# A down projection's first chunk with seven block products for eight, in a hybrid decoder layer

## The chip, the cores and the metric

The kernel runs on one core of one Trainium2 chip. The metric is the device time of one execution in microseconds, the median of several runs. TensorE multiplies, VectorE, ScalarE and GpSimd compute beside it, and DMA moves data; SP's and GpSimd's queues issue the loads spoken of here.

## The reference, cut to what matters

One layer of a decoder: a mixer with state space and mLSTM heads, a cross attention over a memory, and a SwiGLU feed-forward, each between two RMS norms, for 512 prompt tokens and 8 x 8 sample tokens that share the weights. The change lies in the feed-forward:

```python
u = _rms(x) * g_pre_ffn
f = (jax.nn.silu(u @ w_gate) * (u @ w_up)) @ w_down
x = x + _rms(f) * g_post_ffn
```

`u` is 576 tokens by 1024, the hidden width is 2816 (22 tiles of 128), and the output has 1024 columns (8 tiles of 128).

## The kernel before, in words

**Numbers.** Every fp32 operand is split into a high part of reduced precision (`whi`, `hh`, `u3h`) and a low part, the rest (`wlo`, `hl`, `u3l`). A product of two operands is three matmuls of 128x128 weights: high by high, high by low, low by high. Tokens are the moving side, in two halves: 320 and 256 (HALVES), or twice 288 (EHALVES, `E`).

**Hidden tiles.** `H`, then `stores[...]`, holds hidden tiles (gate times up) as high and low parts. Tiles 0 to 3 are computed one by one inside an order written out by hand: a list of steps with positions (`at_(position, step, ...)`), sorted and issued in that order under `manual_schedule` (L2036 to L2051). `silu` (L1682), `times` (L1685) and `hidden` (L1688) are their last steps, in the scratch tile `ct`.

**Seven products for eight.** From tile 4 on, two neighbouring tiles are made together (`Pair`, L1853). The inner dimension is cut into two blocks, the two tiles are the two row blocks, the two token halves the two column blocks, and the 2x2 block product is done with seven block products instead of eight (class `Seven`, L1769, Winograd's form of Strassen's scheme). The weights need sums and differences on VectorE (`sums`, `diffs`) and their splits (`high1`, `parts2`, `parts3`, `parts4`); for two of the factors the low part is made by ScalarE (minus the raw weights) and an accumulating DMA from GpSimd's queue that adds them to the rounded ones (`low`, L1790; `place3`). Products are issued in three steps: `early`, `mid` and, behind the next pair's `early`, `late`. Between them ScalarE copies a PSUM bank (`cc`, `ct`) before a further product is accumulated into it.

**Buffers.** Raw weights have two buffers each for the first and the second tile (`raw`, `rawx`), the high and low parts three each (`whi`, `wlo`), the accumulated low parts two (`wacc`), weight sums one (`sw`). A load goes out when its buffer's last readers are done.

**Down projection, in four chunks of hidden tiles.** `Down` (L1939) does two output tiles with seven products over six hidden tiles (768 columns, blocks of three tiles), from the block sums that `Hidden.put` and `Hidden.sums` (L1924, L1928) made of the hidden tiles; `add` (L1947) adds each product to `f2`. The chunks of tiles 4 to 9 and 10 to 15 go this way. The last chunk (tiles 16 to 21) and **the first one (tiles 0 to 3)** are plain products: `down_chunk` (L1998) over eight output tiles and two token halves, weights split by `split_w` (L171; cast L179, subtraction L186), evacuated by `ev_first` (L2016, copy L2018).

**Order around the change.** By hand: tiles 0 to 3, and gate and up of tiles 4 and 5 up to `mid` of up (`pp`, positions 19 to 28.5). Then, by the order of the program and a scheduler that places instructions on each engine's queue (it may move later steps ahead on an engine): the first chunk with `late` of the pair, gate and up of tiles 6, 7 and 8, 9, gate of 10, 11, four Downs of tiles 4 to 9, up of 10, 11, and so on. Each engine works its queue in order.

Of the kernel before, what the change touches and what calls it, by code (L numbers as in the profile page):

```python
# [11 lines left out]
F32 = mybir.dt.float32  # L12
# [7 lines left out]
P = 128  # L20
# [95 lines left out]
def build(nc, tc, ctx, I, O):  # L116
# [13 lines left out]
    def SL(slot, name, dt=F32, shape=(P, KT, T)):  # L130

        return big.tile(list(shape), dt, name=name, tag="s%d" % slot, bufs=1)
# [56 lines left out]
    def split(hi, lo, src, eng=None, cast=None):  # L189
        c = (cast or A.copy)(hi, src)  # L190
        (eng or V).tensor_tensor(lo, src, hi.bitcast(F32), op=ALU.subtract)  # L191
        return c
# [843 lines left out]
    def SL0(name, dt=F32R):  # L1036
        return big0.tile([P, KT, T], dt, name=name, tag="s0", bufs=1)
# [639 lines left out]
    at_(12.9, S.dma_start, x_d, x)  # L1677


    H = []  # L1680

    def silu(j, i):  # L1682
        A.activation(ct[:, (j + i) % 2, :], B[("g", j), i], AF.Silu)

    def times(j, i):  # L1685
        V.tensor_tensor(ct[:, (j + i) % 2, :], ct[:, (j + i) % 2, :], B[("u", j), i], op=ALU.mult)

    def hidden(j, i):  # L1688
        if not H:
            H.extend((SL0("hh0"), SL(2, "hl0", F32R)))  # L1690
        split(H[0][:, j, E[i]], H[1][:, j, E[i]], ct[:, (j + i) % 2, :])

    def half_tile(*ms):

# [208 lines left out]
    class Hidden:  # L1903
# [19 lines left out]

        def put(s, j, a, i, g):  # L1924
            if (a, i) != (0, 1):
                split(*s.place((j - 4) // 2 % 3, {(0, 0): 4, (1, 0): 5, (1, 1): 6}[a, i]), g)

        def sums(s, j):  # L1928
            q, g = (j - 4) // 2 % 3, gates(j)
            for out, p, m in ((g[0][0], g[0][1], g[0][0]), (g[0][1], g[1][1], g[0][1]), (g[1][1], g[1][1], g[0][0]),  # L1930
                              (g[1][0], g[1][0], g[1][1])):
                V.tensor_tensor(out, p, m, op=ALU.subtract)
            hi, lo = [t_[:, (8, 0)[q]:(8, 0)[q] + 4, :] for t_ in s.b] if q < 2 else [s.rest()[:, 0:4, :], s.rest()[:, 4:8, :]]
            split(hi, lo, gt[:, 4 * (j // 2 % 2):4 * (j // 2 % 2) + 4, :])

        def block(s, m):
            return [[s.place(q, m)[e] for q in range(3)] for e in range(2)]

    class Down(Seven):  # L1939

        def __init__(s, j, k0, hid):
            s.j, s.hid, s.name = j, hid, "dn"
            s.weights_of(I["wdown"][j, :, k0:k0 + 768], I["wdown"][j + 1, :, k0:k0 + 768], 1 - j // 2 % 2)

        def add(s, a, i, ps):
            o = f2[:, s.j + a, E[i]]
            V.tensor_tensor(o, o, ps, op=ALU.add)  # L1947

        def early(s):
            s.x, s.z, y = s.bank(), s.bank(), s.bank()  # L1950
# [62 lines left out]
            m = down_part(nk, j, i, p, w_of(j), n1 if n_ < 3 else 0, nk) if n_ > 2 or n1 < nk else None  # L2013
            evac(n_, j, i, p, m)

    def ev_first(n_, j, i, ps, m):  # L2016
        t0, n = HALVES[i]
        A.copy(f2[:, j, t0:t0 + n], ps)  # L2018


    pp, stores = [], []

    def first_pair(up):
        if not up:
            stores.append(Hidden(*H))
        pp.append(Pair(4, up, stores[0].put, (lambda: stores[0].sums(4)) if up else None))

    for n_ in range(2):
# [1 line left out]
    for p, n_, step in ((19.05, 0, "load"), (19.1, 1, "load"), (21.9, 0, "sums"), (22.05, 0, "high1"), (22.6, 0, "diffs"),  # L2030
                        (23.0, 0, "place3"), (23.05, 0, "parts2"), (23.9, 1, "sums"), (24.1, 0, "parts3"),
                        (23.62, 0, "parts4"), (24.48, 0, "early"), (24.97, 1, "high1"), (25.0, 0, "mid"),
                        (25.4, 1, "diffs"), (26.05, 1, "parts2"), (26.48, 1, "early"), (27.5, 0, "late"),
                        (26.45, 1, "place3"), (26.47, 1, "parts4"), (28.1, 1, "parts3"), (28.5, 1, "mid")):
        at_(p, lambda n_, step: getattr(pp[n_], step)(), n_, step)
    plan.sort()  # L2036
    with tc.manual_schedule(engines={TE.engine, A.engine, V.engine, G.engine, S.engine}):
        for p, _, fn in plan:
# [10 lines left out]
        for p, _, fn in plan:  # L2049
            if p > 19.02:  # L2050
                fn()  # L2051
    hh, hl = H
    f2 = SL(4, "f_ffn")


    firsts = {}

    def w_first(j):
        if j not in firsts:
            with tc.issue_after(pp[0].ev3.ins) if j < 2 else ExitStack():  # L2060
                raw = wp.tile([P, 1024], F32, name="raw", tag="raw", bufs=2)
                for k in (j, j + 1):
                    firsts[k] = split_w(I["wdown"][k, :, 0:512], 512, 512, raw=raw[:, 512 * (k - j):512 * (k - j) + 512])
        return firsts[j]

    down_chunk(4, [(j, i) for j in range(8) for i in (1, 0)], pp[1], w_first, ev_first, 4)
    seq.extend(pp)
    last = run([pair(j, up, stores[0]) for j in (6, 8) for up in range(2)], None)

    def downs(k0, store):  # L2070
        return [lambda j=j: Down(j, k0, store) for j in (0, 2, 4, 6)]

    class Plain:
        def __init__(s, hh, hl):
            s.b = hh, hl

        def put(s, j, a, i, g):
            split(*[t_[:, j % 8, E[i]] for t_ in s.b], g)


    for n_, j0 in enumerate((10, 16)):
        store = stores[-1]
        last = run([lambda: Pair(j0, 0, None)] + downs(512 + 768 * n_, store), last)
        stores.append((Plain if n_ else Hidden)(SL0("hh%d" % n_), SL(2, "hl%d" % n_, F32R)))
        last = run([pair(j0, 1, stores[-1])] + [pair(j, up, stores[-1]) for j in (j0 + 2, j0 + 4) for up in range(2)], last)
    hh, hl = stores[-1].b
    tps.close()
    ph = ctx.enter_context(tc.tile_pool(name="rows2", bufs=1, side="right", reuse_waits="tile"))
# [178 lines left out]
def pack(inp):  # L2267
    i = {k: np.asarray(v) for k, v in inp.items()}
    f = np.float32
    out = {}  # L2270
    x = np.concatenate([i["x_prompt"].reshape(TP, 1024), i["x_sample"].reshape(TS, 1024)], 0)
    out["xT"] = _feat(x)
    out["memT"] = _feat(i["mem_prompt"].reshape(256, 1024))
    par = np.zeros((P, NPAR), f)
    s = {k: par[:, a:b] for k, (a, b) in _cols.items()}
    for k, n in (("g_pre", "g_pre_mix"), ("g_mem", "g_mem"), ("g_ssm", "g_ssm_out"), ("g_ml", "g_mlstm_out"),
                 ("g_pmix", "g_post_mix"), ("g_prex", "g_pre_x"), ("g_postx", "g_post_x"), ("g_preffn", "g_pre_ffn"),
                 ("g_postffn", "g_post_ffn")):
# [24 lines left out]
    out["wxo"] = _units(i["w_xo"][0], KT)  # L2303
    out["wgate"] = _units(i["w_gate"][0], KT)
    out["wup"] = _units(i["w_up"][0], KT)

    w = _units(i["w_down"][0], NFFN)
    taken = [0, 1, 2, 3] + [j + k for j in (4, 10) for k in (0, 2, 4, 1, 3, 5)] + list(range(16, 22))
    out["wdown"] = np.ascontiguousarray(w.reshape(8, P, NFFN, P)[:, :, taken].reshape(w.shape))
    cs = i["state_conv"][0].reshape(NB, 3, 12, P)[:, :, order]  # L2310
    out["convst"] = np.ascontiguousarray(cs.transpose(3, 2, 0, 1))
    out["h0"] = np.ascontiguousarray(i["state_ssm"][0].transpose(0, 3, 1, 2))
    c0 = np.zeros((NB, P, 4, 258), f)
    c0[..., 0:256] = i["state_mlstm_c"][0].transpose(0, 2, 1, 3)
    c0[..., 256] = i["state_mlstm_n"][0].transpose(0, 2, 1)
    out["c0"] = c0
    kc = i["cache_mem_k"][0].reshape(NB, 256, 4, 2, P)
    out["kc"] = np.ascontiguousarray(kc.transpose(0, 4, 3, 2, 1))
    vc = i["cache_mem_v"][0].reshape(NB, 2, P, 4, 256)
    out["vc"] = np.ascontiguousarray(vc.transpose(0, 2, 1, 3, 4))  # L2320
    return out
# [34 lines left out]
```

## Time and profile before

| | |
|---|---|
| median of 3 runs | 1095.19 us (1095.19 to 1096.24) |
| profiled execution | 1096.77 us |
| its span, first to last instruction | 1095.0 us |
| mean granted TensorE clock | 0.998 |
| chain that ended last: TensorE, VectorE, ScalarE, DMA | 88%, 5%, 4%, 2% |
| DMA | 182.29 MB, 166 GB/s over the span |

The profile is one execution. Engines are PE (matmul), PEld (weight load), DVE (VectorE), ACT (ScalarE), POOL (GpSimd) and SP. A row of a group names line, engine, operation, output and inputs by the program's tile names, and shape; a row in order of time begins with start and duration, and ends, in brackets, with the engine's idle time before it and what ended it. Matmuls are pipelined, so their durations overlap.

### The profile page before, as it was taken

The numbers are of one execution on the slowest core, as the hardware profiler recorded it, in microseconds if no ns is written. First come the engines' busy times: TensorE is split into PE (matmuls) and PEld (weight loads), VectorE is DVE, ScalarE is ACT, GpSimd is POOL, SyncE is SP. The second block draws the span as 40 slices with busy tenths as digits, with TensorE's granted clock in tenths as the row PEclk, the third lists the DMA queues.
The fourth block names the chain that finished last, engine by engine and source line by source line (L and its number), as shares of the span: only waits on it lengthen the run. The fifth ranks groups of instructions, "written<-read, shape, count | busy, mean of one in ns | idle before, by whom it ended". The sixth has DMA issues, their size and how long they took to land.

```text
span 1095.0 us, 20715 instructions
## 1 busy us (share of the span) xinstructions
PE 1084.1 (99%) x8124; PEld 1027.5 (94%) x8124; DVE 754.0 (69%) x1507; ACT 611.7 (56%) x1098; POOL 225.8 (21%) x305
## 2 busy tenths in 40 slices
PE   9999999999999999999999999999999999999997
PEld 8999887778999999999988879999999999999997
DVE  6896785658877775558744546676566877787555
ACT  7767632455654555656545445645566566656653
POOL 1332643313213112000144301100011121111000
PEclk9999999999999999999999999999999999999999
DMA  6785635435655349653467775644386687588532
GB/s 204 170 154 127 170 111 174 163 84 177 189 149 146 106 132 312 205 189 102 150 215 271 264 248 163 217 161 109 104 195 142 150 196 173 116 188 186 128 130 88
DMA packets 58967, 182.29 MB, mean 166 GB/s; under 512 B 6605, under 2 KB 11853, under 8 KB 58357
## 3 DMA queue, kind: packets, MB, share of 16 engines
q1 hardware_dynamic: 42740, 138.06, 39.0%
q0 software_dynamic: 15552, 41.95, 19.8%
q8 instruction: 64, 1.05, 0.4%
q10 hardware_dynamic: 576, 0.95, 0.3%
q14 instruction: 35, 0.28, 0.1%
HBM read 160.28 MB, written 20.65 MB: 165 GB/s over the span
## 4 chain that ended last, share of the span: by engine, by line
PE 88%; DVE 5%; ACT 4%; DMA 2%; issue 1%; SPq 0%; POOL 0%; DVEq 0%; ACTq 0%
PE ps_v L814 5%; PE ps_in L202 4%; PE ps_in L201 4%; PE ps_in L204 4%; PE ps_o L202 3%; PE ps_o L204 3%; PE ps_o L201 3%; PE ps_g L1848 3%; PE ps_g L1849 3%; PE ps_g L1850 3%; PE ps_u L1848 3%; PE ps_u L1850 3%; PE ps_u L1849 3%; PE ps_dn L1848 2%; PE ps_dn L1849 2%; PE ps_dn L202 2%
## 5 line engine op out<-in xcount | busy, mean ns | idle before, releaser
L201 PE MATMUL ps_in<-uh,whi 128*128 128x320 f32 (+1 forms) x544 | 164.0, 302 | 0.4 <-DVE cb L450 0.4
L204 PE MATMUL ps_in<-uh,wlo 128*128 128x320 f32 (+1 forms) x544 | 163.2, 300 | 0.0
L202 PE MATMUL ps_in<-ul,whi 128*128 128x320 f32 (+1 forms) x544 | 162.7, 299 | 0.0
L179 ACT CAST whi<-raw 128x1024 fp32r<-128x1024 f32 (+1 forms) x104 | 105.2, 1013 | 96.2 <-PE ps_in L202 26.1
L186 DVE TENSOR_TENSOR wlo<-raw,whi 128x512 fp32r<-128x512 f32 (+1 forms) x96 | 96.6, 1009 | 66.5 <-ACT whi L179 65.8
L201 PEld LDWEIGHTS ps_in<-uh,whi 128*128 128x128 f32 x544 | 103.1, 190 | 3.4 <-issue 1.7
L204 PEld LDWEIGHTS ps_in<-uh,wlo 128*128 128x128 f32 x544 | 103.0, 190 | 1.2 <-issue 0.4
L202 PEld LDWEIGHTS ps_in<-ul,whi 128*128 128x128 f32 x544 | 103.1, 190 | 0.6
L184 POOL DMA_DIRECT2D wlo<-win x32 | 27.9, 871 | 80.1 <-ACT wlo L183 72.0
L1848 PE MATMUL ps_g<-b,whi 128*128 128x288 f32 x144 | 42.5, 295 | 0.0
L1849 PE MATMUL ps_g<-b,whi 128*128 128x288 f32 x144 | 42.4, 295 | 0.0
L1848 PE MATMUL ps_u<-b,whi 128*128 128x288 f32 x144 | 42.4, 295 | 0.0
L1849 PE MATMUL ps_u<-b,whi 128*128 128x288 f32 x144 | 42.4, 295 | 0.0
L1821 ACT CAST whi<-rawx 128x1024 fp32r<-128x1024 f32 (+1 forms) x26 | 25.7, 987 | 27.8 <-PE ps_dn L1849 13.8
L191 DVE TENSOR_TENSOR wlo<-sw,whi 128x1024 fp32r<-128x1024 f32 (+1 forms) x26 | 29.6, 1140 | 14.9 <-ACT whi L190 14.7
L201 PE MATMUL ps_xo<-qh,whi 128*128 128x288 f32 x128 | 38.5, 302 | 0.2 <-ACT whi L179 0.2
L202 PE MATMUL ps_o<-mixs_l,whi 128*128 128x320 f32 (+1 forms) x128 | 38.2, 299 | 0.0
L204 PE MATMUL ps_o<-mixm_h,wlo 128*128 128x256 f32 (+1 forms) x128 | 38.2, 298 | 0.0
L202 PE MATMUL ps_o<-mixm_l,whi 128*128 128x256 f32 (+1 forms) x128 | 37.9, 296 | 0.0
L201 PE MATMUL ps_xq<-u2h,whi 128*128 128x320 f32 (+1 forms) x128 | 37.9, 300 | 0.0
L201 PE MATMUL ps_o<-mixm_h,whi 128*128 128x256 f32 (+1 forms) x128 | 37.9, 296 | 0.0
L204 PE MATMUL ps_xq<-u2h,wlo 128*128 128x320 f32 (+1 forms) x128 | 37.9, 296 | 0.0
(765 smaller groups left out, 3838.9 us busy)
## 6 DMA issues: line engine op xcount, KB each, us to landing
raw<-win SPq DMA_DIRECT2D x35, 512.0 KB, 3.9
raw<-wout SPq DMA_DIRECT2D x17, 512.0 KB, 3.6
raw<-wxq SPq DMA_DIRECT2D x13, 512.0 KB, 3.6
raw<-wgate SPq DMA_DIRECT2D x13, 512.0 KB, 3.5
raw<-wup SPq DMA_DIRECT2D x13, 512.0 KB, 5.3
wlo<-win POOLq DMA_DIRECT2D x24, 256.0 KB, 5.1
kva<-kc SPq DMA_DIRECT2D x12, 512.0 KB, 5.7
kva<-vc SPq DMA_DIRECT2D x12, 512.0 KB, 6.0
```

Source lines behind the costliest of these rows:

```text
L179: casts.append(A.copy(hi[:, :n], raw[:, :n]))
L184: G.dma_start(lo[:, a:b], src[:, a:b], accum_op=ALU.add)
L186: e.tensor_tensor(lo[:, a:b], raw[:, a:b], hi[:, a:b].bitcast(F32), op=ALU.subtract)
L191: (eng or V).tensor_tensor(lo, src, hi.bitcast(F32), op=ALU.subtract)
L201: mm(ps, wh, ah, start=i == 0, stop=False)
L202: mm(ps, wh, al, start=False, stop=False)
L204: m = mm(ps, tiles[order[c]][1], xh(order[c], t0, n), start=False, stop=c == len(tiles) - 1)
L814: mm(ps, a, b, skip_group_check=True, **kw)
L1821: A.copy(s.h3[:, s.all], s.r2[:, s.all])
L1848: mm(ps, wh, b[0][k], start=start and k == 0, stop=False, skip_group_check=True)
L1849: mm(ps, wh, b[1][k], start=False, stop=False, skip_group_check=True)
L1850: m = mm(ps, wl, b[0][k], start=False, stop=k == nk - 1, skip_group_check=True)
```

## The change

The first chunk is done by `Down` too, with blocks of two hidden tiles (0 and 2 in the first, 1 and 3 in the second; 512 columns of weights). So it comes behind the gate of tiles 6 and 7, and its `late` steps lie in front of and among the up products of these.

- Tiles 0 to 3 need block sums. Their second halves are written by `times` to a tile `tf` (tiles 0 and 1) or to the idle half of the gates' tile `gt` (tiles 2 and 3) by `single`; `hidden` splits three of four halves, since the scheme has no use for the fourth by itself.
- `first_sums` makes the four sums of a pair of tiles in six VectorE operations (the first halves are put together again from high and low part), and `first_parts` splits them (128x1152). They are put by hand at 24.6 and 26.04 for tiles 0 and 1, and at 28.3 and 28.6 for tiles 2 and 3.
- Places in the store rotate: tiles 4, 5 now have the third place (`te`), 6, 7 and 8, 9 the first and second; the weights' order in memory follows.
- The first product into an output block is copied by ScalarE instead of added.
- `down_chunk`'s first call, `w_first`, `ev_first` and `firsts` go.

```diff
     def times(j, i):
-        V.tensor_tensor(ct[:, (j + i) % 2, :], ct[:, (j + i) % 2, :], B[("u", j), i], op=ALU.mult)
+        V.tensor_tensor(single(j) if i else ct[:, (j + i) % 2, :], ct[:, (j + i) % 2, :], B[("u", j), i], op=ALU.mult)
 
     def hidden(j, i):
-        split(H[0][:, j, E[i]], H[1][:, j, E[i]], ct[:, (j + i) % 2, :])
+        if (j % 2, i) != (0, 1):
+            split(*stores[0].place(j // 2, {(0, 0): 4, (1, 0): 5, (1, 1): 6}[j % 2, i]), single(j) if i else ct[:, (j + i) % 2, :])
...
+        def first_sums(s, q):
+            t_ = tf[0] if q == 0 else gt[:, 4:8, :]
+            g = [[t_[:, 2 * a + i, :] for i in range(2)] for a in range(2)]
+            (h11, l11), (h21, l21) = [[b.bitcast(F32) for b in s.place(q, m)] for m in (4, 5)]
+            for out, p, m, op in ((g[0][0], g[0][1], h11, ALU.subtract), (g[0][0], g[0][0], l11, ALU.subtract),
+                                  (g[0][1], g[1][1], g[0][1], ALU.subtract), (g[1][1], g[1][1], g[0][0], ALU.subtract),
+                                  (g[1][0], h21, g[1][1], ALU.subtract), (g[1][0], g[1][0], l21, ALU.add)):
+                V.tensor_tensor(out, p, m, op=op)
+
+        def first_parts(s, q):
+            split(*[t_[:, (8, 0)[q]:(8, 0)[q] + 4, :] for t_ in s.b], tf[0][:, 0:4, :] if q == 0 else gt[:, 4:8, :])
...
         def add(s, a, i, ps):
             o = f2[:, s.j + a, E[i]]
-            V.tensor_tensor(o, o, ps, op=ALU.add)
+            if (s.j, a, i) in begun:
+                V.tensor_tensor(o, o, ps, op=ALU.add)
+            else:
+                begun.add((s.j, a, i))
+                A.copy(o, ps)
...
+    for q, p, d in ((0, 24.6, 26.04), (1, 28.3, 28.6)):
+        at_(p, lambda q: stores[0].first_sums(q), q)
+        at_(d, lambda q: stores[0].first_parts(q), q)
...
-    down_chunk(4, [(j, i) for j in range(8) for i in (1, 0)], pp[1], w_first, ev_first, 4)
-    last = run([pair(j, up, stores[0]) for j in (6, 8) for up in range(2)], None)
...
+    for j0, j1, k0, n in ((6, 10, 0, 512), (10, 16, 512, 768), (16, NFFN, 1280, 768)):
+        store = stores[-1]
+        last = run([pair(j0, 0, store)] + downs(k0, n, store), last)
```

More of the change, by code (lines that the diff above doesn't have):

```diff
@@ L1677, in build, with single @@
     at_(12.9, S.dma_start, x_d, x)
-    H = []
+    stores, tf = [], []
+    def single(j):
+        if j < 2:
+            if not tf:
+                tf.append(tp.tile([P, 9, 288], F32, name="tf", tag="te"))
+            return tf[0][:, 2 * j + 1, :]
+        return gates(6)[j % 2][1]
     def silu(j, i):
@@ L1685, in times @@
     def times(j, i):
-        V.tensor_tensor(ct[:, (j + i) % 2, :], ct[:, (j + i) % 2, :], B[("u", j), i], op=ALU.mult)
+        V.tensor_tensor(single(j) if i else ct[:, (j + i) % 2, :], ct[:, (j + i) % 2, :], B[("u", j), i], op=ALU.mult)
     def hidden(j, i):
-        if not H:
-            H.extend((SL0("hh0"), SL(2, "hl0", F32R)))
-        split(H[0][:, j, E[i]], H[1][:, j, E[i]], ct[:, (j + i) % 2, :])
+        if not stores:
+            stores.append(Hidden(SL0("hh0"), SL(2, "hl0", F32R)))
+        if (j % 2, i) != (0, 1):
+            split(*stores[0].place(j // 2, {(0, 0): 4, (1, 0): 5, (1, 1): 6}[j % 2, i]), single(j) if i else ct[:, (j + i) % 2, :])
     def half_tile(*ms):
@@ L1925, in put @@
             if (a, i) != (0, 1):
-                split(*s.place((j - 4) // 2 % 3, {(0, 0): 4, (1, 0): 5, (1, 1): 6}[a, i]), g)
+                split(*s.place(j // 2 % 3, {(0, 0): 4, (1, 0): 5, (1, 1): 6}[a, i]), g)
+        def first_sums(s, q):
[8 more added lines that the diff above has]
+            split(*[t_[:, (8, 0)[q]:(8, 0)[q] + 4, :] for t_ in s.b], tf[0][:, 0:4, :] if q == 0 else gt[:, 4:8, :])
         def sums(s, j):
-            q, g = (j - 4) // 2 % 3, gates(j)
+            q, g = j // 2 % 3, gates(j)
             for out, p, m in ((g[0][0], g[0][1], g[0][0]), (g[0][1], g[1][1], g[0][1]), (g[1][1], g[1][1], g[0][0]),
@@ L1937, in block, with __init__ @@
             return [[s.place(q, m)[e] for q in range(3)] for e in range(2)]
+    begun = set()
     class Down(Seven):
-        def __init__(s, j, k0, hid):
+        def __init__(s, j, k0, n, hid):
             s.j, s.hid, s.name = j, hid, "dn"
-            s.weights_of(I["wdown"][j, :, k0:k0 + 768], I["wdown"][j + 1, :, k0:k0 + 768], 1 - j // 2 % 2)
+            s.weights_of(I["wdown"][j, :, k0:k0 + n], I["wdown"][j + 1, :, k0:k0 + n], 1 - j // 2 % 2)
         def add(s, a, i, ps):
             o = f2[:, s.j + a, E[i]]
-            V.tensor_tensor(o, o, ps, op=ALU.add)
+            if (s.j, a, i) in begun:
[3 more added lines that the diff above has]
+                A.copy(o, ps)
         def early(s):
@@ L2014, in down_chunk @@
             evac(n_, j, i, p, m)
[L2016 to L2021, printed above, removed]
+    pp = []
     def first_pair(up):
-        if not up:
-            stores.append(Hidden(*H))
         pp.append(Pair(4, up, stores[0].put, (lambda: stores[0].sums(4)) if up else None))
@@ L2051, in build, with downs @@
                 fn()
-    hh, hl = H
     f2 = SL(4, "f_ffn")
[L2056 to L2064, printed above, removed]
-    down_chunk(4, [(j, i) for j in range(8) for i in (1, 0)], pp[1], w_first, ev_first, 4)
     seq.extend(pp)
-    last = run([pair(j, up, stores[0]) for j in (6, 8) for up in range(2)], None)
-    def downs(k0, store):
-        return [lambda j=j: Down(j, k0, store) for j in (0, 2, 4, 6)]
+    last = pp[1]
+    def downs(k0, n, store):
+        return [lambda j=j: Down(j, k0, n, store) for j in (0, 2, 4, 6)]
     class Plain:
@@ L2077, in put @@
         def put(s, j, a, i, g):
-            split(*[t_[:, j % 8, E[i]] for t_ in s.b], g)
-    for n_, j0 in enumerate((10, 16)):
+            split(*[t_[:, j - 16, E[i]] for t_ in s.b], g)
+    for j0, j1, k0, n in ((6, 10, 0, 512), (10, 16, 512, 768), (16, NFFN, 1280, 768)):
         store = stores[-1]
-        last = run([lambda: Pair(j0, 0, None)] + downs(512 + 768 * n_, store), last)
-        stores.append((Plain if n_ else Hidden)(SL0("hh%d" % n_), SL(2, "hl%d" % n_, F32R)))
-        last = run([pair(j0, 1, stores[-1])] + [pair(j, up, stores[-1]) for j in (j0 + 2, j0 + 4) for up in range(2)], last)
+        last = run([pair(j0, 0, store)] + downs(k0, n, store), last)
+        if j0 > 6:
+            stores.append((Plain if j1 == NFFN else Hidden)(SL0("hh%d" % j0), SL(2, "hl%d" % j0, F32R)))
+        last = run([pair(j0, 1, stores[-1])] + [pair(j, up, stores[-1]) for j in range(j0 + 2, j1, 2) for up in range(2)], last)
     hh, hl = stores[-1].b
@@ L2307, in pack @@
     w = _units(i["w_down"][0], NFFN)
-    taken = [0, 1, 2, 3] + [j + k for j in (4, 10) for k in (0, 2, 4, 1, 3, 5)] + list(range(16, 22))
+    taken = [0, 2, 1, 3] + [j + k for k in range(2) for j in (6, 8, 4)] + [j + k for k in range(2) for j in (12, 14, 10)] + list(range(16, 22))
     out["wdown"] = np.ascontiguousarray(w.reshape(8, P, NFFN, P)[:, :, taken].reshape(w.shape))
```

## The prediction

> **What bounds the kernel now.** I read the page first, then the busy time by stretches, then TensorE's own instructions in order of time, and last what VectorE, ScalarE and the load queue do beside them.
>
> ```profile
> span 1095.0 us, 20715 instructions
> PE 1084.1 (99%) x8124; PEld 1027.5 (94%) x8124; DVE 754.0 (69%) x1507; ACT 611.7 (56%) x1098; POOL 225.8 (21%) x305
> PEclk9999999999999999999999999999999999999999
> ```
>
> TensorE is busy in 99% of the span and its clock is granted in full in every slice. So what counts is its number of matmuls, and any place where it would have to wait. The stretches of the stage (PE, PEld, DVE, ACT, POOL, granted clock, DMA share, GB/s; the first chunk of the down projection begins near 769) say the same:
>
> ```profile
> 750.00:769.00 19.00, 19.00 (x144) 18.86 (x143) 10.99 (x19) 10.10 (x19) 0.85 (x1) 1.00 0.39 105
> 769.00:790.00 21.00, 21.00 (x160) 21.00 (x159) 12.03 (x21) 10.86 (x22) 0.86 (x1) 1.00 0.31 95
> 790.00:828.00 38.00, 38.00 (x291) 38.00 (x290) 20.83 (x35) 25.89 (x44) 6.88 (x8) 1.00 0.85 187
> ```
>
> VectorE and ScalarE are busy for a little over half of the time, DMA for a third: there is room beside the matmuls, but not without limit. TensorE's instructions in order of time (start, duration) give the price of one matmul:
>
> ```profile
> 752.91 0.29 PE L1850 MATMUL ps_g<-u3h,wacc 128*128 128x288 f32 x1
> 753.11 0.40 PE L1848 MATMUL ps_g<-b,whi 128*128 128x288 f32 x1
> ...
> 761.17 0.29 PE L1848 MATMUL ps_g<-b,whi 128*128 128x288 f32 x1
> 764.34 0.29 PE L1848 MATMUL ps_u<-b,whi 128*128 128x288 f32 x1
> ...
> 767.53 0.30 PE L1848 MATMUL ps_u<-b,whi 128*128 128x288 f32 x1
> ```
>
> From 761.17 to 764.34 lie two products of 12 matmuls: 3.17 us, so 0.132 us each from start to start. The 0.29 us is the length of one, which overlaps the next. The mean of 0.3 us per matmul in the page's groups must not be multiplied by a count.
>
> **The saving.** The old chunk issues 8 output tiles x 2 halves x 4 hidden tiles x 3 terms = 192 matmuls of 320 or 256 columns (288 on average); the new one 4 pairs x 7 products x 2 x 3 = 168 of 288 columns. The built program has 24 matmuls fewer in all. 24 x 0.132 = **3.17 us** less on the engine that sets the end.
>
> The Trainium skill ("TensorE: Matmul & The Clock Gate", the start-to-start rule for a warm array) gives N / 2.4 GHz + 2.5 ns, 122.5 ns for 288 columns as an estimate; the row has 132, and by the rule the saving would be 2.9 us.
>
> **What it adds on VectorE and ScalarE.** Removed: the splits of the second halves of tiles 0 and 2 (each a cast of 0.43 and a subtraction of 0.46), and the eight casts and eight subtractions of 512 columns of the old weights. The sixteen evacuating copies on ScalarE stay sixteen, of 288 columns. Added: twelve 288-column sums (six for each pair of tiles), two splits of 128x1152, and per Down seven steps on weights and three adds on VectorE, and four to six steps on weights on ScalarE. All of this costs nothing as long as TensorE isn't kept waiting, so I look at each place where a TensorE instruction depends on it. The order of the built program gives the neighbours, the rows the durations. VectorE (what ended an idle time stands in brackets):
>
> ```profile
> 753.30 0.46 DVE L1867 TENSOR_TENSOR gt<-ps_g,cc 128x288 f32<-128x288 f32 x1
> 758.64 0.46 DVE L1867 TENSOR_TENSOR gt<-ps_g,cc 128x288 f32<-128x288 f32 x1 [4.88 <-ACT cc L1892]
> ...
> 760.54 1.22 DVE L191 TENSOR_TENSOR wlo<-sw,whi 128x1024 fp32r<-128x1024 f32 x1 [0.25 <-ACT whi L190]
> 761.69 0.68 DVE L191 TENSOR_TENSOR wlo<-d,u3h 128x512 fp32r<-128x512 f32 x1
> 762.29 0.68 DVE L1803 TENSOR_TENSOR sw<-rawx 128x512 f32<-128x512 f32 x1
> 762.89 0.45 DVE L1872 TENSOR_TENSOR ct<-ps_u,cc 128x288 f32<-128x288 f32 x1
> ...
> 764.34 0.46 DVE L191 TENSOR_TENSOR hl<-gt,hh 128x288 fp32r<-128x288 f32 x1 [0.50 <-ACT hh L190]
> 764.71 0.45 DVE L1867 TENSOR_TENSOR gt<-ps_g,ct 128x288 f32<-128x288 f32 x1
> ...
> 780.76 1.36 DVE L191 TENSOR_TENSOR hl<-gt,hh 128x1152 fp32r<-128x1152 f32 x1 [0.63 <-ACT hh L190]
> ```
>
> ScalarE in the same time:
>
> ```profile
> 752.33 0.43 ACT L190 CAST hh<-ct 128x288 fp32r<-128x288 f32 x1 [1.33 <-DVE ct L1686]
> 752.67 0.39 ACT L1881 COPY cc<-ps_g 128x288 f32<-128x288 f32 x1
> ...
> 759.13 0.44 ACT L1868 ACTIVATE gt<-gt 128x288 f32<-128x288 f32 x1 [0.53 <-DVE gt L1867]
> 759.48 1.03 ACT L190 CAST whi<-sw 128x1024 fp32r<-128x1024 f32 x1
> ...
> 765.20 0.45 ACT L1868 ACTIVATE gt<-gt 128x288 f32<-128x288 f32 x1 [0.58 <-DVE gt L1867]
> 765.55 1.03 ACT L1821 CAST whi<-rawx 128x1024 fp32r<-128x1024 f32 x1
> 766.49 0.39 ACT L1888 COPY ct<-ps_u 128x288 f32<-128x288 f32 x1
> ...
> 779.57 1.16 ACT L190 CAST hh<-gt 128x1152 fp32r<-128x1152 f32 x1
> ```
>
> Step by step:
>
> 1. *First six sums, tiles 0 and 1.* They stand between the two rows of L1867, in 4.88 us of idle time; six of at most 0.5 us take 3. Cost 0. The cast of tile 2's second half (752.33) falls away ahead of the copy at 752.67, so TensorE's small gap at 752.91 to 753.35 (two intervals of 0.20 and 0.24 for 0.13, so 0.18 us) goes; but ScalarE then scales tiles 6 and 7's gate weights (1024 columns, about 1 us) ahead of the next copy out of the same bank, and by the same count some 0.2 us comes back there. Net 0; it would be 0.2 either way. Those weights are loaded in the place of the first down weights:
>
> ```profile
> 748.33 0.89 SPq L174 DMA_DIRECT2D raw<-wdown  x2
> ```
>
> One 512 KB load instead of two of 256 KB, landed by 754 at the longest, while ScalarE comes to it near 755; the accumulating load behind it has until 770. Nothing on SP's or POOL's queue waits longer for it.
>
> 2. *First split, 128x1152.* It stands ahead of the casts of the up weights of tiles 4 and 5, in both queues. ScalarE: 759.48 + 1.16 = 760.64. VectorE then: split to 761.97 (1.36, the next starts 0.09 earlier), low half of the sum weights 1.15, of the fourth weights 0.60, so 763.72. Behind it now stand ct 0.37, tiles 6 and 7's first weight sum 0.60 (also there before), gt 0.37, **their second sum and difference 0.60 + 0.60 (moved up here from behind the old chunk)**, hl 0.37, and gt 0.45: 767.08 instead of 765.16. ScalarE is held with it: activation 0.35, cast 0.94, copy 0.39, so 768.8 instead of 766.88. The product of up that begins at 767.53 adds to the bank which this copy reads, so it has to wait: 1.3 us, and some 0.1 more for its third term, whose weights VectorE makes behind the cast. **Stall A, 1.4 us.** Before, this place had 0.65 us to spare. Lower bound 0 (if the order by waits were looser than I read it), upper 2.0.
>
> 3. *Second six sums and split.* They come after that product, and the first Down needs them only behind four products of tiles 4 to 7 (12 matmuls each, 6.3 us). Counted through as above they are ready before the first Down begins. Cost 0; without this cover their 2.7 + 2.5 us would show.
>
> 4. *Downs.* One Down is now 42 matmuls, 5.5 us, instead of 63 and 8.3 us for those of 768 columns; its loads, casts and low halves are smaller in proportion, but landing times are not. Going through the waits of the first three Downs I find each weight ready 0.4 us or more ahead of its product. The tight place is the fourth Down. There VectorE's queue has the first sum of tiles 6 and 7's up weights (it waits for a 512 KB load) ahead of the low half of the fourth Down's own sum weights. The load can be issued only when the third Down has released the buffer, one 288-sized step after the add behind the second Down's last product.
>
> ```profile
> DMA to landing us min/median/max: 3.2/3.9/5.9
> ```
> ```profile
> rawx<-wup SPq DMA_DIRECT2D x9, 512.0 KB, 3.5
> wacc<-wup POOLq DMA_DIRECT2D x9, 512.0 KB, 6.1
> ```
>
> The first line is that of the rawx loads from 840 to 900, the others the median per kind. From the start of that product's last matmul: 0.29 (its end) + 0.37 (add) + 0.45 (low half) + 3.9 (load) + 0.60 (sum) + 0.37 (add) + 0.37 (low half, 256 columns, taken as 288) + 0.60 (difference) + 0.69 (low half, 512 columns) = 7.6 us. TensorE has 53 matmuls until it needs the last of these: 7.0 us. **Stall B, 0.6 us**; 0 with a load of 3.2, 2.6 with one of 5.9. The accumulating load of the same up weights (6.1) comes out 0.3 to 0.7 late at the product behind it, which falls into the same stall. I take 0.7.
>
> The Trainium skill ("DMA: Bandwidth & Descriptors", the section on the fixed cost) has 2.0 us + bytes / 436 GB/s: 3.2 us for 512 KB, as an estimate. That is the least of the rows; by it stall B is nil and the sum 1.8 us faster.
>
> 5. *Behind the chunk* the order of the pairs and Downs is nearly that of before; the hidden tiles' places rotate, which I cost at 0, within 0.3 either way.
>
> Sum: -3.17 + 1.4 + 0.7 = **-1.1 us**. The profiled execution took 1096.77 us, 1.8 more than its span; the median of the runs is 1095.19. One like the profiled would take about 1095.7; for the median I predict 1094.1.
>
> **Rivals.**
> - *No stall: the whole saving.* For it: TensorE had next to no gap in this stretch, the Downs of 768 columns run the same way, and the sums were put where VectorE idles. Against it: stall A follows from queue order. Time 1095.19 - 3.17 = 1092.0.
> - *The short Downs are bound by their preparation.* Per Down ScalarE needs about 4.1 us (four steps of 0.52, two of 0.33, four copies of 0.33) and VectorE about 3.8 of TensorE's 5.5, in queues that stand still for a buffer or a load several times. If each Down waits 1.1 us for its first weights, as one load landing in 5.9 instead of 3.9 would do to the places where I find 0.4 to 0.8 us to spare, four cost 4.4; with stall A it is 5.8 - 3.17 = 2.6 us slower, 1097.8. It makes the kernel slower from 3.2 us of stalls on, and by over 0.2% from 5.4 on. Against it: the same steps for 768 columns left stalls of a few tenths. The Trainium skill ("TensorE: Matmul & The Clock Gate", Part 1) halves the clock after an idle window of about 3.4 us; no row here shows one.
> - *That the products aren't fewer* is excluded by the program itself.
>
> **How the numbers follow.** 0.2% is 2.2 us (1093.0 and 1097.4), about what a measurement can tell from no change. Forecast 1094.1, its own range 1093.0 to 1096.3 (stall B from 0 to 2.6, A to 2.0), 0.60; no stall, 1092.0, 0.20; slower, 1097.8, 0.20. Range: 1091.9 to 1097.0, which leaves out most of the last case. Faster 0.22 (the second case and the lower edge of the first), same 0.60, slower 0.18.
>
> **What would show it.** The same granted clock and 24 matmuls fewer at 0.132 us. Stall A: a gap of about 1.4 us ahead of the fifth product of the up weights of tiles 4 and 5, ended by ScalarE's copy behind a cast; no gap there means step 2 is wrong. Stall B: TensorE waiting in the fourth Down, at its third product in the order of issue, for a VectorE low half, with VectorE idle before a sum from rawx, released by a DMA. Gaps at the start of every Down would speak for the slower rival; a difference after the chunk, where I put none, would make the sum wrong altogether.

## The result, and the profile after

The changed kernel takes **1097.86 us** in the median (22 runs, 1096.53 to 1100.17), the kernel before 1095.61 in 22 runs beside them (1094.98 to 1097.09). The ratio is 1.002 with a 95% interval of 1.0013 to 1.0026: 2.2 us slower. I had predicted 1094.1, within 1091.9 to 1097.0. The sign was wrong, and the time lies 0.9 us outside the range.

The profiled execution of the changed kernel took 1096.94 us, near the fastest of its runs; that of before, 1096.77, was near the slowest of its own. And ahead of the change, at a step that both have (713.41 and 712.54 us), the execution of before is already 0.87 us behind. So this pair of spans shows less of the loss than the medians do. The page of after, its first part and the granted clock:

```profile
span 1095.2 us, 20777 instructions
...
PE 1082.0 (99%) x8100; PEld 1024.4 (94%) x8100; DVE 768.5 (70%) x1551; ACT 619.8 (57%) x1114; POOL 232.4 (21%) x313
...
PEclk9999999999999999999999999999999999999999
```

The 24 matmuls are gone (8124 to 8100), the clock is as before, and TensorE is busy for 2.1 us less while the span hasn't shrunk. So TensorE waits more. The busy time by stretches of after (PE, PEld, DVE, ACT, POOL, clock, DMA share, GB/s) answers to the three rows of before:

```profile
750.00:769.00 19.00, 17.82 (x131) 17.22 (x130) 14.29 (x27) 11.30 (x21) 2.55 (x3) 1.00 0.56 117
769.00:790.00 21.00, 21.00 (x161) 21.00 (x160) 17.48 (x39) 15.30 (x30) 4.26 (x5) 1.00 0.59 126
790.00:828.00 38.00, 37.09 (x279) 36.73 (x278) 28.98 (x59) 28.27 (x53) 8.62 (x10) 1.00 0.85 203
```

TensorE lost 1.2 us in the first stretch and 0.9 in the third; before it lost nothing in any of them. VectorE has 14.3 and 17.5 us of work in the first two, for 11.0 and 12.0. The view of TensorE's waits from 745 to 1055 (what was waited for: total, times, longest) has three rows for after; for the kernel before it has none:

```profile
PE ps_dn L1858 <- ACT whi L190: 1.2, 2, 0.6
PE ps_u L1858 <- ACT ct L1898: 1.1, 1, 1.1
PE ps_dn L1860 <- DVE wlo L191: 0.9, 1, 0.9
```

The second row is the predicted stall A, the third the predicted stall B. The first, two waits in a Down, was not predicted; I call it **C**. In order of time, TensorE at A, B and the first of the two C:

```profile
766.70 0.29 PE L1860 MATMUL ps_u<-b,wlo 128*128 128x288 f32 x1
768.09 0.40 PE L1858 MATMUL ps_u<-b,whi 128*128 128x288 f32 x1 [1.09 <-ACT ct L1898]
768.32 0.29 PE L1859 MATMUL ps_u<-b,whi 128*128 128x288 f32 x1
...
802.32 0.29 PE L1859 MATMUL ps_dn<-hl,whi 128*128 128x288 f32 x1
803.51 0.40 PE L1860 MATMUL ps_dn<-hh,wlo 128*128 128x288 f32 x1 [0.91 <-DVE wlo L191]
...
857.85 0.42 PE L1858 MATMUL ps_dn<-hh,whi 128*128 128x288 f32 x2
858.85 0.40 PE L1858 MATMUL ps_dn<-hh,whi 128*128 128x288 f32 x1 [0.58 <-ACT whi L190]
859.09 0.30 PE L1859 MATMUL ps_dn<-hl,whi 128*128 128x288 f32 x1
```

The bracket has the time for which the engine stood empty. The loss is larger, since matmuls overlap: from 766.70 to 768.09 are 1.39 us where 0.13 would do, 1.26 lost, and the next interval has another 0.1. Below, a gap is always this: the difference of starts beyond 0.132 per matmul, with the late intervals right behind it. So A is 1.46 us, B 1.17, and C 0.95 at 858.85 (0.1 of it two microseconds later, at 861.09) and as much again at 959.89, where the kernel before had 0.32 at each of the two places.

A second profiled execution of the same kernel (the run "again" below, 1099.39 us) has a fourth wait:

```profile
PE ps_dn L1858 <- ACT whi L190: 1.2, 2, 0.6
PE ps_u L1858 <- ACT ct L1898: 1.1, 1, 1.1
PE ps_dn L1860 <- DVE wlo L191: 1.0, 1, 1.0
PE ps_u L1860 <- DMA wacc<-wup: 1.0, 1, 1.0
```

The last row is **D**, 1.30 us: the first up product of tiles 6 and 7, at 808.84, waits for the accumulating load of its weights. D comes and goes with the landing time of that load: 5.2 us in the first trace, 7.5 in "again". That fits the spread of the changed kernel's runs, 3.6 us for 2.1 of before.

### The profile page after: what moved, and what is told of

The parts are those of the page before. It is cut to its first block, busy times and chain, and to the rows that moved or that the text cites. A ratio compares the mean times of both kernels' runs of the same rounds, so it can differ in the third digit from the quotient of the medians.

```text
span 1095.2 us, 20777 instructions
## 1 busy us (share of the span) xinstructions
PE 1082.0 (99%) x8100; PEld 1024.4 (94%) x8100; DVE 768.5 (70%) x1551; ACT 619.8 (57%) x1114; POOL 232.4 (21%) x313
## 4 chain that ended last, share of the span: by engine, by line
PE 84%; DVE 6%; ACT 4%; issue 3%; DMA 2%; POOL 0%; DVEq 0%; SPq 0%; ACTq 0%; POOLq 0%
PE ps_in L202 4%; PE ps_in L201 4%; PE ps_in L204 4%; PE ps_v L814 3%; PE ps_o L202 3%; PE ps_o L204 3%; PE ps_o L201 3%; PE ps_g L1858 3%; PE ps_g L1859 3%; PE ps_g L1860 3%; PE ps_u L1858 3%; PE ps_u L1860 3%; PE ps_u L1859 3%; PE ps_dn L1858 2%; PE ps_dn L1860 2%
## 5 line engine op out<-in xcount | busy, mean ns | idle before, releaser
L179 ACT CAST whi<-raw 128x1024 fp32r<-128x1024 f32 x96 | 100.2, 1045 | 90.9 <-PE ps_in L202 26.4
L186 DVE TENSOR_TENSOR wlo<-raw,whi 128x1024 fp32r<-128x1024 f32 (+1 forms) x88 | 91.1, 1038 | 63.5 <-ACT whi L179 62.9
L1858 PE MATMUL ps_dn<-hh,whi 128*128 128x288 f32 x160 | 46.6, 297 | 1.2 <-ACT whi L190 1.2
L1859 PE MATMUL ps_dn<-hl,whi 128*128 128x288 f32 x160 | 46.6, 294 | 0.0
L1831 ACT CAST whi<-rawx 128x1024 fp32r<-128x1024 f32 (+2 forms) x30 | 28.1, 936 | 27.7 <-PE ps_dn L1859 14.9
L1973 DVE TENSOR_TENSOR f_ffn<-f_ffn,ps_dn 128x288 f32<-128x288 f32 x68 | 30.3, 451 | 17.4 <-PE ps_dn L1860 14.6
L191 DVE TENSOR_TENSOR wlo<-sw,whi 128x1024 fp32r<-128x1024 f32 (+2 forms) x30 | 32.4, 1080 | 11.8 <-ACT whi L190 10.8
L1810 ACT CAST whi<-raw 128x1024 fp32r<-128x1024 f32 (+2 forms) x30 | 28.0, 935 | 20.7 <-PE ps_dn L1859 10.0
```

Of the source, the lines that this page charges most:

```text
L179: casts.append(A.copy(hi[:, :n], raw[:, :n]))
L186: e.tensor_tensor(lo[:, a:b], raw[:, a:b], hi[:, a:b].bitcast(F32), op=ALU.subtract)
L1831: A.copy(s.h3[:, s.all], s.r2[:, s.all])
L1858: mm(ps, wh, b[0][k], start=start and k == 0, stop=False, skip_group_check=True)
L1859: mm(ps, wh, b[1][k], start=False, stop=False, skip_group_check=True)
```

## The experiments

Theory 1: the saving of 3.17 us is there, and waits at fixed places (A, B and C) eat it. Theory 2, the rival: the loss lies in loads that land at different times. Each kernel was run beside the kernel before. The gaps are worked out from the starts in one profiled execution each; B is the sum over the fourth Down, C that at both places, "before" the median of the kernel before as it stood with that run (35, 35 and 21 runs).

| kernel | median, us | before | ratio, 95% | A | B | D | C |
|---|---|---|---|---|---|---|---|
| again (the changed kernel) | 1097.58 | 1096.11 | 1.0006 to 1.0023 | 1.46 | 1.32 | 1.30 | 1.92 |
| places | 1096.38 | 1096.11 | 0.9991 to 1.0008 | 1.48 | 1.42 | 0.95 | 0.65 |
| hold_a | 1097.99 | 1096.11 | 1.0008 to 1.0025 | 0.79 | 0.69 | 1.76 | 1.92 |
| hold_b | 1097.80 | 1096.11 | 1.0008 to 1.0025 | 1.48 | 0 | 1.25 | 1.91 |
| order_before | 1097.57 | 1096.05 | 1.0005 to 1.0022 | 0 | 0 | 0 | 1.90 |
| hold_a2 | 1097.19 | 1096.05 | 1.0004 to 1.0021 | 0.87 | 0.6 | 0.1 | 1.91 |
| halves | 1095.65 | 1096.05 | 0.9988 to 1.0005 | 1.48 | 0.4 | 0 | 1.91 |
| all4 | 1093.65 | 1096.05 | 0.9972 to 0.9989 | 0.86 | 0.2 | 0 | 0.64 |
| halves_only | 1096.92 | 1095.85 | 1.0000 to 1.0018 | 1.46 | 1.5 | 0 | 1.90 |
| all5 | 1093.53 | 1095.85 | 0.9969 to 0.9987 | 0.39 | 0.2 | 0 | 0.65 |

**again.** The changed kernel as it is.

> The changed kernel once more, as the measure for the three others. Theory 1 (the saving of 3.17 us is there and three waits of TensorE eat it: A ahead of the fifth product of up of tiles 4 and 5, 1.5 us; B in the fourth Down, 1.1 to 1.3; C in the first Down of the second and of the third chunk, about 0.6 more each than before): a median near 1097.9, the same gaps at the same four places. Theory 2 (the loss lies in loads that land at different times, so in gaps that wander from one execution to the next, B above all): other gaps in this profile than in the first, B anywhere from 0 to 2.6 us.

A and C were the same to a few hundredths, B within 0.15; D was new, 1.30 us. So theory 1 has three of the losses, theory 2 a fourth.

**places: the newest hidden tiles last.** The order of the three places inside each product of the six-tile chunks:

```diff
-            return [[s.place(q, m)[e] for q in range(3)] for e in range(2)]
+            return [[s.place(q, m)[e] for q in ((0, 1) if n == 256 else (2, 0, 1))] for e in range(2)]
...
-    taken = [...] + [j + k for k in range(2) for j in (6, 8, 4)] + [j + k for k in range(2) for j in (12, 14, 10)] + [...]
+    taken = [...] + [j + k for k in range(2) for j in (4, 6, 8)] + [j + k for k in range(2) for j in (10, 12, 14)] + [...]
```

> Only the order of the hidden tiles inside each product of the six-tile chunks is changed: the pair that is made last is multiplied last again (places 2, 0, 1 instead of 0, 1, 2, with the weights' rows put in that order). Theory 1: the gaps in the first Down of the second and third chunk fall from 0.95 to about 0.3 us each, 1.2 us less, a median near 1096.6; A and B stay. Theory 2 and a rival of C (the gap comes from the short first chunk ahead of it, by buffers that come free at other times): the gaps stay, time as the changed kernel within 0.3 us.

C fell from 1.92 to 0.65 us, and the median by 1.2, as theory 1 had it. TensorE's waits of this kernel no longer have a row for the cast of L190:

```profile
PE ps_u L1858 <- ACT ct L1898: 1.1, 1, 1.1
PE ps_u L1860 <- DMA wacc<-wup: 0.7, 1, 0.7
PE ps_dn L1860 <- DVE wlo L191: 0.7, 1, 0.7
PE ps_dn L1858 <- ACT f_ffn L1976: 0.2, 1, 0.2
```

**order_before: that order alone, in the kernel before.** The converse, with nothing else of the change:

```diff
-            return [[s.place(q, m)[e] for q in range(3)] for e in range(2)]
+            return [[s.place(q, m)[e] for q in (1, 2, 0)] for e in range(2)]
...
-    taken = [0, 1, 2, 3] + [j + k for j in (4, 10) for k in (0, 2, 4, 1, 3, 5)] + list(range(16, 22))
+    taken = [0, 1, 2, 3] + [j + k for j in (4, 10) for k in (2, 4, 0, 3, 5, 1)] + list(range(16, 22))
```

> The kernel before, with one thing alone: inside each product of the six-tile chunks the pair of hidden tiles that is made last is multiplied second, as in the changed kernel, where it was multiplied last (places 1, 2, 0 for 0, 1, 2, the weights' rows put in that order). If the place of the newest tiles is all that makes gap C: the gaps in the first Down of both six-tile chunks rise from 0.3 to about 0.95 us, and the kernel before gets 1.2 us slower, 1097.1 to 1097.3. If gap C needs the short first chunk ahead of it: no change beyond 0.3 us.

It cost 1.5 us (0.5 to 2.4 by the interval), the two gaps grew by 1.26, and TensorE's waits show the very row of the changed kernel:

```profile
PE ps_dn L1848 <- ACT whi L190: 1.2, 2, 0.6
```

How C comes about is seen with what TensorE has to do beside the cast. The sum weights' cast (ScalarE, L190) is written into a `whi` buffer that TensorE has just read, and both rows put its start down to TensorE; the first row below is ScalarE in the kernel before, the second in the changed one:

```profile
859.85 0.83 ACT L190 CAST whi<-sw 128x768 fp32r<-128x768 f32 x1 [0.65 <-PE ps_dn L1849]
```
```profile
857.96 0.83 ACT L190 CAST whi<-sw 128x768 fp32r<-128x768 f32 x1 [0.39 <-PE ps_dn L1859]
```

And TensorE in the kernel before at this place:

```profile
859.59 0.30 PE L1850 MATMUL ps_dn<-hh,wacc 128*128 128x288 f32 x1
859.73 0.42 PE L1848 MATMUL ps_dn<-te,whi 128*128 128x288 f32 x2
859.99 0.29 PE L1849 MATMUL ps_dn<-te,whi 128*128 128x288 f32 x1
860.12 0.30 PE L1850 MATMUL ps_dn<-te,wlo 128*128 128x288 f32 x1
860.25 0.29 PE L1849 MATMUL ps_dn<-te,whi 128*128 128x288 f32 x1
860.39 0.29 PE L1850 MATMUL ps_dn<-te,wlo 128*128 128x288 f32 x1
860.73 0.40 PE L1848 MATMUL ps_dn<-hh,whi 128*128 128x288 f32 x1
```

Both casts take 0.83 us. Before, six matmuls (0.8 us) of the newest tiles, in the place `te`, lie beside it. In the changed kernel only the two at 857.85 do (0.26 us): the newest tiles are multiplied second, their low parts aren't ready (VectorE, below, makes them until 858.63), and the scheduler has put the product that needs the cast ahead of the rest.

```profile
857.27 1.36 DVE L191 TENSOR_TENSOR hl<-gt,hh 128x1152 fp32r<-128x1152 f32 x1
```

0.5 us of cover is gone at each place, and the gap grew by 0.6.

**hold_a: the sums of tiles 6 and 7's gate weights held.** On VectorE, behind the low half of the up weights of tiles 4 and 5 (`v3`, the subtraction of `parts3`):

```diff
+            if isinstance(p, Pair) and p.j == 6 and not p.up:
+                p.hold = pp[1].v3
...
         def sums(s):
+            with s.held():          # tc.issue_after(s.hold.ins), where hold is set
                 V.tensor_tensor(sw[:, s.LB], s.r2[:, s.LA], s.r2[:, s.LB], op=ALU.add)
                 V.tensor_tensor(sw[:, s.LA], sw[:, s.LB], s.r1[:, s.LA], op=ALU.subtract)
```

> VectorE's sums and differences of tiles 6 and 7's gate weights are held behind the low half of the up weights of tiles 4 and 5, so that ScalarE's cast and copy come earlier. Theory 1: gap A falls from 1.5 us to 0.2 or less, a median near 1096.5, about 1.4 less than the changed kernel; B and C stay. Rival (the split of 128x1152 alone makes the copy late): 0.5 us less at most. If the held steps come late for tiles 6 and 7's gate themselves, a new gap shows near 773.

A miss: A fell only to 0.79, and 0.66 came up at 782 (the fourth row), in the gate of tiles 6 and 7, where ScalarE's copy of a bank now stood behind a cast of Down weights. TensorE's waits of this kernel:

```profile
PE ps_u L1865 <- DMA wacc<-wup: 1.5, 1, 1.5
PE ps_dn L1863 <- ACT whi L1822: 1.2, 2, 0.6
PE ps_u L1863 <- ACT ct L1903: 0.4, 1, 0.4
PE ps_g L1863 <- ACT ct L1903: 0.4, 1, 0.4
PE ps_dn L1865 <- DVE wlo L1823: 0.2, 1, 0.2
```

The rest of A is ScalarE's. In the trace of after a further step of tiles 6 and 7's gate, the scaled copy for their fourth weights, had also slipped ahead, and ScalarE stood still for its buffer in front of it; the cast behind it feeds VectorE, and that the gate:

```profile
763.84 0.63 ACT L1805 ACTIVATE wlo<-rawx 128x512 fp32r<-128x512 f32 x1 [1.63 <-PE ps_g L1860]
764.42 0.43 ACT L190 CAST hh<-gt 128x288 fp32r<-128x288 f32 x1
...
766.36 0.45 ACT L1878 ACTIVATE gt<-gt 128x288 f32<-128x288 f32 x1 [1.19 <-DVE gt L1877]
766.71 1.03 ACT L1831 CAST whi<-rawx 128x1024 fp32r<-128x1024 f32 x1
767.64 0.39 ACT L1898 COPY ct<-ps_u 128x288 f32<-128x288 f32 x1
```

**hold_a2: one step on each engine held, and less long.** VectorE's second sum only behind the sum that ends the gate of tiles 4 and 5 (`v1`), ScalarE's scaled copy behind that gate's activation (`a1`):

```diff
+                p.hold, p.hold_c = pp[0].v1, pp[0].a1
...
+            with s.held(s.hold):
                 V.tensor_tensor(sw[:, s.LA], sw[:, s.LB], s.r1[:, s.LA], op=ALU.subtract)
...
+            with s.held(s.hold_c):
                 s.low(s.l3[:, s.LA], s.r2[:, s.LB], s.src2[:, s.LB], s.made[1])
```

> The changed kernel with two steps of tiles 6 and 7's gate weights held: VectorE's second sum and its difference only behind the sum that ends the gate of tiles 4 and 5, and ScalarE's scaled copy for the fourth weights behind the activation of the same gate. The first form of this edit left 0.7 us of gap A, because ScalarE stood still for that scaled copy, and put 0.7 us at 782. Theory 1 (two steps that slipped ahead, one on each engine, make gap A): gap A at 0.3 us or less and nothing new at 782, a median 1.2 to 1.4 below the changed kernel. Rival (the wide split makes it): 0.7 us or more of gap A is left.

Nothing new at 782, but 0.87 us of A were left, and the median was 0.4 below that of "again", a third of what was expected. By its number that was the rival's case. What is left had a plainer reason: VectorE's first sum and the first difference of those weights, 0.6 us each, still stood ahead of the gate, which all5 tests.

**hold_b: the sums of tiles 6 and 7's up weights held** behind the low half of the fourth Down's sum weights (`v2`, the subtraction of `parts2`):

```diff
+            if isinstance(p, Pair) and p.j == 6 and p.up:
+                p.hold = seq[-1].v2
```

> VectorE's first sums of tiles 6 and 7's up weights are held behind the low half of the fourth Down's own sum weights. Theory 1: gap B falls from 1.1 us to 0.3 or less, a median 1.0 to 1.3 below the changed kernel's. Theory 2 (the landing of that load makes the spread of the changed kernel's runs, 1096.5 to 1100.2): 2 us or more below it in the median, and a spread as narrow as that of the kernel before (2.1 us).

B went, and the kernel gained nothing: 1097.80 against 1097.58, and a spread of 4.3 us. The time came back one product later, as D:

```profile
PE ps_dn L1863 <- ACT whi L1822: 1.2, 2, 0.6
PE ps_u L1863 <- ACT ct L1903: 1.1, 1, 1.1
PE ps_u L1865 <- DMA wacc<-wup: 1.0, 1, 1.0
```

Both theories missed here: B was cover for D. While TensorE stands at B, the accumulating load goes on landing, and without B TensorE stands for it one product later.

**halves: hold_b, and that load in two parts.** The accumulating load of tile 6's up weights, with its scaled copy, as two of 256 KB instead of one of 512, the half that is needed first going first:

```diff
-                s.low(s.l1[:, s.all], s.r1[:, s.all], s.src1, s.made[0])
+                for c in (s.LA, s.LB) if isinstance(s, Pair) and s.j == 6 and s.up else (s.all,):
+                    s.low(s.l1[:, c], s.r1[:, c], s.src1[:, c], s.made[0])
```

> The changed kernel with the sums of the fourth Down held as before (which took gap B away and left 1.2 us at the product behind it, gap D), and with the accumulating load of the up weights of tile 6 issued in two halves of 256 KB, so that the half that is needed first lands earlier. If B and D are one lateness, that of a chain of two loads (512 KB, then the accumulating one of 512 KB, 5.6 and 6.4 to 7.5 us), both gaps go: a median 2.0 to 2.5 below the changed kernel, and narrower runs. If the load queues are short of bandwidth there (DMA share 0.9 to 0.98), the halves land no earlier: D stays near 1.2 us and the time is that of the changed kernel.

B and D both went, the median fell by 1.9 us against "again", and the runs spread over 2.3 us instead of 2.7 to 4.3. The loads from 795 to 812, in "again" and then in "halves":

```profile
wacc<-wup POOLq DMA_DIRECT2D x1, 512.0 KB, 7.5
```
```profile
wacc<-wup POOLq DMA_DIRECT2D x2, 256.0 KB, 5.5
```

**halves_only: the two parts without the held sums.**

> The changed kernel with the accumulating load of tile 6's up weights in two halves and nothing else; VectorE's queue order in the fourth Down is as in the changed kernel. If B (VectorE standing behind the first of the two loads) and D (the landing of the second) are separate waits: B stays at 0.8 to 1.3 us and D goes, a median near 1096.7, about 1 below the changed kernel. If the halves also speed the load that B waits for (issued ahead of them, so it should not): B falls too, and the time comes near 1095.7.

D went, B stayed (1.5 us), and the median was 0.7 below that of "again". So B and D are separate waits, for two loads that don't depend on each other (B's is `rawx`, the second tile's weights; D's adds to a copy made from `raw`, the first's), and both have to go for the gain of 1.9.

**all4: places, hold_a2, hold_b and halves together.**

> All edits at once: the newest tiles multiplied last, the two held steps of tiles 6 and 7's gate weights, the held sums of the fourth Down, the accumulating load in halves. If the saving of 3.17 us is real and the waits A (1.4), B and D (2.0 to 2.5) and C (1.2) are all that ate it: 1097.7 - 4.6 to 5.1 = 1092.6 to 1093.1, that is 2.7 to 3.2 us faster than the kernel before in the same call. If some other loss stays (the wider use of VectorE and of the loads), 1094 or more.

1093.65 us, 2.4 below the kernel before and 3.9 below the changed one, with runs within 1.3 us. The forecast was missed by 0.6 us. Left was 0.86 of A, the one row that TensorE's waits still have:

```profile
PE ps_u L1866 <- ACT ct L1906: 0.5, 1, 0.5
```

**all5: more of the held steps.** As all4, with both sums behind `v1` and both differences behind `v3`:

```diff
+            with s.held(s.hold_b or s.hold):
                 V.tensor_tensor(sw[:, s.LB], s.r2[:, s.LA], s.r2[:, s.LB], op=ALU.add)
...
+            with s.held(s.hold_d):          # pp[1].v3
                 V.tensor_tensor(s.r2[:, s.LA], s.r1[:, s.LA], s.r2[:, s.LA], op=ALU.subtract)
```

> All edits at once, and more of tiles 6 and 7's gate weights held: both VectorE sums behind the sum that ends the gate of tiles 4 and 5, both differences behind the low half of the up weights. In the kernel with all edits so far gap A was still 0.87 us, and VectorE's first sum and a difference (0.6 us each) still stood ahead of that gate. If these two steps make the rest of A: A at 0.3 us or less, and 0.5 to 0.8 us less in the median, 1092.9 to 1093.2. If the wide split makes it: A stays near 0.8 us and the time at 1093.65. If the held steps come late for their own product, a new gap near 780 and no gain.

A fell to 0.39 us and no wait is left in that view, but the median, 1093.53, is only 0.1 below that of all4 (1092.65 to 1094.5 against 1093.33 to 1094.61). The ratio is 0.9978 (0.9969 to 0.9987): this version is faster than both kernels. Its gaps from 720 to 1060 sum to 2.25 us, those of the kernel before to 1.44; 3.17 less the difference of 0.8 is 2.4, and 2.3 were measured.

What executions differ by ahead of the change can be taken out: all twelve traces have six narrow matmuls ahead of it, and a wait of TensorE in the last chunk, behind it. In all5:

```profile
712.59 0.72 PE L1582 MATMUL ps_ss<-c,ssq 128*128 128x1 f32 x6
...
1043.80 0.41 PE L204 MATMUL ps_dn<-hh,wdl 128*128 128x320 f32 x1
```

From start to start this stretch lasts 333.60 us in the kernel before, 334.73 in the first trace of the changed kernel, 336.04 in "again", 331.69 in all4 and 331.21 in all5. So in the profiled executions all5 is 0.48 us faster than all4, as much as A fell, though the medians show only 0.1. Less the gaps inside it, the stretch is 332.6 us in the kernel before, 332.8 in order_before, and 329.4 to 329.6 in all ten traces of the changed kernel and its variants. So the saving, 3.0 to 3.3 us, is there in each of them, and the gaps are what ate it.

## Why the prediction was wrong, point by point

- *The saving, 3.17 us*: right; the stretch without its gaps is 3.0 to 3.3 us shorter.
- *Step 1, net 0*: nearly. The gap ahead of gate's fifth product is 0.36 us instead of 0.18, so 0.2 us lost, the "0.2 either way" of the text.
- *Step 2, stall A, 1.4 us*: right in place, releaser and size (1.46). The cause named there, steps that moved ahead on VectorE, holds with an addition: all5, where A falls to 0.39, also holds a step of the same weights for which ScalarE stood still, and that one I had not seen. The wide split makes 0.39 of A at most.
- *Step 3, cost 0*: right; from 769 to 790 TensorE is busy throughout.
- *Step 4, stall B, 0.7 us*: right in place and kind; **its size failed.** I took 3.9 and 6.1 us for the two loads; the first took 4.5, the second 5.2 to 7.5. With 4.5 the sum of this step gives 1.2, which is what B measured (1.17 and 1.32). And I let the second fall "into the same stall", while it comes behind it. In "again" B and D are 2.6 us together, the upper end that I had worked out for B, and 1.2 in the first profile.

The first load in "again", as SP's queue issues it, and as VectorE, released by it, goes on 4.5 us later:

```profile
797.49 0.33 SPq L1793 DMA_DIRECT2D rawx<-wup  x1
```
```profile
801.98 0.69 DVE L1813 TENSOR_TENSOR sw<-rawx 128x512 f32<-128x512 f32 x1 [3.14 <-DMA rawx<-wup]
```

I had taken 3.9 us from 840 to 900 of the kernel before, where the DMA engines' share (next to last column) is 0.75. Where the two loads land in "again", in the second row, it is 0.90:

```profile
840.00:900.00 60.00, 59.95 (x453) 59.71 (x452) 48.33 (x96) 35.39 (x58) 10.36 (x12) 1.00 0.75 167
```
```profile
800.00:810.00 10.00, 7.92 (x57) 7.46 (x56) 5.75 (x12) 8.06 (x16) 2.77 (x4) 1.00 0.90 219
```

The Trainium skill ("DMA: Bandwidth & Descriptors", "Issuing engines are not separate DMA queues") says that loads from all issuing engines run on the same 16 DMA engines and interleave. The 4.5 us agree with that, but the share doesn't settle the landing time: from 800 to 810 of the first trace it is 0.88, and the accumulating load of 7.5 us in "again" landed in 5.2 there. What makes the difference stays open. The 3.2 us that the prediction took from the Trainium skill ("DMA: Bandwidth & Descriptors", the section on the fixed cost) come from a fit there to loads issued by GpSimd; this load of SP's queue took 4.5.

- *Step 5, "the hidden tiles' places rotate, which I cost at 0, within 0.3 either way"*: **this step failed.** It costs 1.3 us in the gaps (1.9 against 0.64), 1.2 by "places" and 1.5 by "order_before". I had read the rotation as a matter of names. It sets which tiles are multiplied last, and the newest ones, multiplied last, were the work that lay beside a cast.
- *The sum*: with the measured sizes it is -3.17 + 0.2 (step 1) + 1.5 (A) + 1.2 to 2.6 (B and D) + 1.3 (C) = +1.0 to +2.4 us. 1.5 and 2.2 were measured in two sets of runs. Against the -1.1 of the forecast that is 1.3 from step 5, 0.5 to 1.9 from step 4, and 0.3 from steps 1 and 2. The time itself is off by 0.4 us more, since I started from 1095.19, the median of 3 runs, and 22 gave 1095.61. The upper edge of my own range, 1096.3, was too low for the bounds it names: with A at 2.0 and B at 2.6 it would be 1096.6.
- *The rivals.* "The short Downs are bound by their preparation" gave 1097.8 and so almost the time, but not the cause: there is no gap at the start of each Down, and of the four short ones only the fourth waits. A late load can add 1.3 us and more (D), but it didn't turn the sign: without D the sum is +1.0 already. "No stall" was wrong for the kernel as written; with the waits taken away most of it is to be had.

I had named "a difference after the chunk, where I put none" as what would make the sum wrong altogether. That is where step 5 failed. The trace of before has the two casts with their cover; I had not read it there.

## What to carry to other kernels

A reordering that is free in the arithmetic is not free in a pipeline: ask of every operand which work the old order put beside its preparation, and count that work again in the new order. Take a load's landing time as a range from more than one trace, and look at every load that the next products wait for: a stall taken away ahead of the last of them may only move the wait there. When a scheduler may move later steps ahead on an engine, most of a saving of 3 us can be lost to steps that nobody needed yet; holding them, splitting one load and putting the order back took 4.1 us off the changed kernel (1097.58 to 1093.53).

## What the runs showed of the hardware that was not expected

- An accumulating load of 512 KB at the same place of nearly the same program landed in 5.2, 6.1, 6.4, 6.8, 7.5 and 7.5 us (after, hold_a2, hold_b, places, again, hold_a); D was 0, 0.1, 1.25, 0.95, 1.30 and 1.76 us (in hold_b without B ahead of it). The two loads of 256 KB by which "halves" replaces it still took 5.5 us in the median: half the bytes, and no less than the quickest of the whole ones.
- After a wait, the next interval between two matmuls' starts is longer too: 768.09 to 768.32 is 0.23 us where 0.13 is usual. So a wait costs some 0.1 us more than the hole itself.
- Executions differ ahead of the change as well: one and the same step, the six narrow matmuls some 55 us ahead of stall A, began between 711.8 and 713.6 us in the twelve traces of this study. That is as much as most effects here, so gaps inside a stage were compared, stretches between two fixed points, and medians of eleven runs and more.
